# A norm's channel weight and rstd in one VectorE operation, and weight splits in four pieces, in a hybrid decoder block

## The chip, the core and the metric

The kernel runs on one core of a Trainium2 chip. The metric is device time in microseconds (us) of one execution. A core has five engines that run their own instruction queues and meet only at semaphores: TensorE (PE) multiplies matrices, VectorE (DVE), ScalarE (ACT) and GpSimd (POOL) work element by element, and SyncE (SP) issues transfers. Data lie in an on-chip memory of 128 partitions (SBUF) and in the accumulators of TensorE (PSUM).

## The reference

One decoder layer on 1024 tokens with 16 learned meta tokens in front (1040 rows of 1024 channels), in float32:

```python
h = jnp.concatenate([meta, x], axis=1)
mix = hybrid_mixer(rms_norm(h, g_pre_mix), w_in, ...)     # short convolution and stick-breaking attention
h = h + rms_norm(mix, g_post_mix)
ffn = conv_gated_mlp(rms_norm(h, g_pre_ffn), ...)
h = h + rms_norm(ffn, g_post_ffn)

def rms_norm(x, g):
    y = xf * lax.rsqrt(jnp.mean(xf * xf, axis=-1, keepdims=True) + RMS_EPS)
    return (y * g).astype(x.dtype)
```

The mixer multiplies the normalised rows by `w_in` (1024 x 8192), which yields the convolution's three inputs, q, k, v of 16 heads and two gates. Attention works on blocks of queries: with z the scaled scores, a weight is sigmoid(z) times the running product, from the query backwards, of 1 - sigmoid(z). The two branches are projected, gated, summed and multiplied by `w_out`. The MLP follows. The change touches the first norm and all products with `w_in` and the two branch projections.

## The kernel before

**Precision by splitting.** TensorE takes a rounded float type (F32R). Each operand is split into a high part, rounded by ScalarE, and a low part, the difference: `split` (L63 to L65) issues a copy on ScalarE (L64) and a subtraction (L65) on VectorE or, where asked, on GpSimd. A product is then three matmuls: high x high, high x low, low x high (L124 to L126). L64 and L65 are lines of a helper, so that in the profile they are told apart by their tiles: `whi`, `wlo` for weights, `ah`, `al` for attention weights, `vv` for values, `xnT` for the normalised rows.

**Dense products.** `Dense` runs a list of 80 items (64 column blocks of `w_in`, 8 of each branch projection). An item has one weight block of 128 x 1024. `load` (L96) fetches it on SP's queue into `raw`, `prep` (L103) splits it into `whi` and `wlo`, with the subtraction on GpSimd, and `run` (L112) does 3 chunks of tokens with 8 x 3 matmuls each; at the start of item i, item i+1 is prepared and the load of i+2 issued. `raw`, `whi` and `wlo` have two buffers each.

**The start.** `x_block(b)` norms 128 rows (the ninth block has 16): ScalarE squares and sums (L456), `rstd_of` (L67 to L77) makes 1/sqrt by a ScalarE square root and five one-column VectorE operations, the rows are weighted (L458 to L462), and `to_features` (L174) transposes them on TensorE (L179) in two groups of four, each split by ScalarE and VectorE into `xnT`. In blocks 0 to 2 the weighting is one VectorE operation, x times rstd times channel weight (L459); in the later blocks GpSimd multiplies by the channel weight (L461) and VectorE by rstd (L462). `start_items` interleaves the blocks with the chunks of the first two items.

**Attention.** For every pair of heads (8 pairs), `stage1` makes scores (L326, L327), two sigmoids on ScalarE (L328, L329), a running product by a VectorE scan over up to 1040 columns (L336), a product on GpSimd (L339), and a causal mask on GpSimd (L340). `stage2` transposes the weights on TensorE (L373), splits them into `ah` (ScalarE) and `al` (VectorE), and multiplies them with `vv` (L363, L364). Steps of the two stages alternate, and between them steps of the dense items are run at a rate that ends them with the pair. The convolution branch has two VectorE operations of 1026 columns per block (`conv3`, L196 to L199).

Each engine's queue is set when the kernel is built, by a scheduler that may move independent instructions past one another, so the order of the queues is near that of the code but not the same. After attention come the projections (to about 1260 us), `w_out` and the second norm, the up-projection and the down-projection, which the diff doesn't touch.

Of the kernel before, what the change touches and what calls it, by code (L numbers as in the profile page):

```python
# [8 lines left out]
F32 = mybir.dt.float32  # L9
F32R = mybir.dt.float32r  # L10
AF = mybir.ActivationFunctionType
ALU = mybir.AluOpType
# [3 lines left out]
D = 1024  # L16
# [16 lines left out]
def block_kernel(ctx, tc, x, meta_tokens, g_pre_mix, w_in, channels, w_proj_conv,  # L33
                 w_proj_attn, w_out, g_post_mix, g_pre_ffn, w_up_gate, w_down,
                 g_post_ffn, out):
    nc = tc.nc

    def pool(name, bufs=1, side="left", space=None):
        kw = dict(name=name, bufs=bufs, reuse_waits="tile")
        if space is not None:  # L40
            kw["space"] = space
        else:
            kw["side"] = side
        return tc.tile_pool(**kw)
# [18 lines left out]
    def split(hi, lo, src, lo_engine=None):  # L63
        nc.scalar.copy(hi, src)  # L64
        (lo_engine or nc.vector).tensor_tensor(lo, src, hi.bitcast(F32), op=ALU.subtract)  # L65

    def rstd_of(small, ssq, n):  # L67
        v = small.tile([P, 1], F32, name="v", tag="v")
        s = small.tile([P, 1], F32, name="s", tag="s")
        t = small.tile([P, 1], F32, name="t", tag="t")  # L70
        v, s, t, ssq = v[:n], s[:n], t[:n], ssq[:n]
        nc.vector.tensor_scalar(v, ssq, 1.0 / D, EPS, op0=ALU.mult, op1=ALU.add)
        nc.scalar.activation(s, v, AF.Sqrt)
        nc.vector.reciprocal(s, s)
        nc.vector.scalar_tensor_tensor(t, s, v, s, op0=ALU.mult, op1=ALU.mult)
        nc.vector.tensor_scalar(t, t, -0.5, 1.5, op0=ALU.mult, op1=ALU.add)
        nc.vector.tensor_tensor(s, s, t, op=ALU.mult)  # L77
        return s

    class Dense:  # L80
# [22 lines left out]
        def prep(self, i):  # L103
            if i < len(self.items) and i not in self.hl:
                self.load(i)
                raw = self.raw.pop(i)
                hi = wpool.tile([P, D], F32R, name="whi", tag="whi")
                lo = wpool.tile([P, D], F32R, name="wlo", tag="wlo")
                split(hi, lo, raw, nc.gpsimd)
                self.hl[i] = (hi, lo)  # L110

        def run(self, i):  # L112
# [61 lines left out]
    def to_features(dst_hi, dst_lo, src, n, pp):  # L174
        for j in range(2):
            tp = pp.tile([P, 512], F32, name="tp", tag="tp")
            for k in range(4):
                kb = 4 * j + k
                nc.tensor.transpose(tp[:, k * P:k * P + n], src[:n, kb * P:(kb + 1) * P],  # L179
                                    ident[:n, :n])  # L180
            tv = tp.rearrange("p (k n) -> p k n", k=4)[:, :, :n]
            split(dst_hi[:, 4 * j:4 * j + 4], dst_lo[:, 4 * j:4 * j + 4], tv)
# [231 lines left out]
    def start_items(x_block):  # L414
        gens = [dense.run(0), dense.run(1)]

        def chunk(i, n):
            for _ in range(n):
                next(gens[i], None)

        for c in range(3):
            for b in range(3):
                x_block(3 * c + b)
                if c > 0 and b < 2:
                    chunk(b, 8)
        chunk(0, 9)
        chunk(1, 9)

    with ExitStack() as p0:
        small = p0.enter_context(pool("p0s", 2, "right"))  # L430
        gb = work.tile([P, NT], F32, name="gb", tag="wk", bufs=4)[:, :D]
        junk = work.tile([P, NT], F32, name="junk", tag="wk", bufs=4)[:, :D]
        warm = small.tile([P, 1], F32, name="warm", tag="v")
        nc.vector.memset(warm, 1.0)
        nc.scalar.activation(warm, warm, AF.Sqrt)

        xts = {}

        def x_load(b):
            n = P if b < 8 else 16  # L440
            xt = work.tile([P, NT], F32, name="xt", tag="be", bufs=6)[:, :D]
            if b == 0:
                nc.sync.dma_start(xt[:NMETA, :], meta_tokens)
                nc.sync.dma_start(xt[NMETA:, :], x[:P - NMETA, :])
            elif b < 9:
                nc.sync.dma_start(xt[:n, :], x[P * b - NMETA:P * b - NMETA + n, :])
            xts[b] = xt

        def x_block(b):
            if b + 3 < 9:  # L450
                x_load(b + 3)
            n = P if b < 8 else 16
            xt = xts[b]
            xn = work.tile([P, NT], F32, name="xn", tag="fl")[:, :D]
            ssq = small.tile([P, 1], F32, name="ssq", tag="ssq")
            nc.scalar.activation((xn if b < 2 else junk)[:n], xt[:n], AF.Square, accum_out=ssq[:n])  # L456
            r = rstd_of(small, ssq, n)
            if b < 3:  # L458
                nc.vector.scalar_tensor_tensor(xn[:n], xt[:n], r, gb[:n], op0=ALU.mult, op1=ALU.mult)  # L459
            else:  # L460
                nc.gpsimd.tensor_tensor(xn[:n], xt[:n], gb[:n], op=ALU.mult)  # L461
                nc.vector.tensor_scalar(xn[:n], xn[:n], r, None, op0=ALU.mult)  # L462
            to_features(xnT[:, 0, :, b * P:b * P + n], xnT[:, 1, :, b * P:b * P + n], xn, n, ps_tp)

        x_load(0)
        nc.sync.dma_start(gb, g_pre_mix.partition_broadcast(P))
        x_load(1)
        x_load(2)
        dense.load(0)
        dense.load(1)  # L470
        nc.sync.dma_start(par, channels[:, :40])
        start_items(x_block)


# [553 lines left out]
    for k, _ in enumerate(products(0, *HALF[1], bank_of(ps_o, "po"), evac_u(*HALF[1]))):  # L1028
        if k % 2:
            next(prep, None)  # L1030
# [40 lines left out]
    for i in range(1, len(pairs)):  # L1071
        p, gate = divmod(i, 2)
        if gate:
            conv_gelu(p)
            sets = [products(i, 1, 512, bank, evac_g(p))]
        else:
            sets = [products(i, j0, n, bank, evac_u(j0, n)) for j0, n in HALF]
        for _ in prep:
            pass
        prep = prep_pair(i + 1) if i < last_pair else prep_down_first()  # L1080
        for si, st in enumerate(sets):
            for k, _ in enumerate(st):
                if gate or (7 * si + k) % 2:
                    next(prep, None)
# [45 lines left out]
    for gi, fbs in enumerate(groups):  # L1130
# [14 lines left out]
        for tb in range(8):  # L1145
# [3 lines left out]
            for hf in range(2):  # L1149
                ps = bank()  # L1150
                c = slice(hf * 512, (hf + 1) * 512)
# [6 lines left out]
                a = accs[tb][:, c]  # L1158
# [4 lines left out]
                if last:  # L1163
                    sq = dw.tile([P, 512], F32, name="sq", tag="sq", bufs=2)
                    nc.scalar.activation(sq, a, AF.Square, accum_out=ssqs[tb][:, hf:hf + 1])
                    eng = nc.vector if (tb == 7 and hf) else nc.gpsimd
                    eng.tensor_tensor(a, a, g_post2[:, c], op=ALU.mult)
            next(prep, None)
            if last:
                a, hb, s0 = accs[tb], hbs[tb], ssqs[tb]  # L1170
                nc.vector.tensor_tensor(s0[:, 0:1], s0[:, 0:1], s0[:, 1:2], op=ALU.add)
                r = rstd_of(fsml, s0[:, 0:1], P)
                for hf in range(2):
                    c = slice(hf * 512, (hf + 1) * 512)
                    nc.vector.scalar_tensor_tensor(a[:, c], a[:, c], r, hb[:, c],
                                                   op0=ALU.mult, op1=ALU.add)
# [58 lines left out]
```

## Time and profile before

| | us |
|---|---|
| median of 3 executions (2069.74 to 2076.77) | 2070.41 |
| the profiled execution | 2079.27 |
| its span, first to last instruction | 2077.1 |
| GpSimd busy (44%) | 914.8 |
| VectorE busy (50%) | 1033.7 |

The profile is of one execution, somewhat longer than the median. A row of its timeline is: start in the span, duration, engine, line, operation, output<-inputs, shapes, count of merged instructions and, in brackets, how long the engine had been idle and what ended that. A group's row gives the busy time of its instructions, the mean of one, and the idle time of the engine before them. A row of the waits is: engine, line, what it waited for, total, times, longest. An instruction that is held up after it has begun counts as busy, so a long duration can be a wait.

### The profile page before, as it was taken

How to read it: one execution, taken by the hardware profiler on the slowest of the kernel's cores; microseconds unless marked ns; L12 is line 12 of the kernel's file. 1: busy time of each engine (PE TensorE's matmuls, PEld its weight loads, DVE VectorE, ACT ScalarE, POOL GpSimd, SP SyncE). 2: the span in 40 equal slices, each digit the busy share in tenths (PEclk: the TensorE clock that was granted, in tenths of full speed). 3: DMA queues.
4: the chain of work that ended last, by engine and by line, in shares of the span. 5: the costliest groups of instructions: out<-in, count | busy, mean ns of one | idle time of the engine just before them, and what ended most of it. 6: DMA issues, size and time to landing. Idle time of an engine off the chain costs nothing.

```text
span 2077.1 us, 30701 instructions
## 1 busy us (share of the span) xinstructions
PE 1988.1 (96%) x12228; PEld 1860.9 (90%) x12228; DVE 1033.7 (50%) x1545; ACT 851.9 (41%) x1771; POOL 914.8 (44%) x764
## 2 busy tenths in 40 slices
PE   5999999999999999999999989979999999999997
PEld 5999999999999999999999989978898899878886
DVE  6445555555555555554232114685444444445546
ACT  4445454545444454545441113354334434412122
POOL 4444444434444444444212551225655656555353
PEclk9999999999999999999999999989999999999999
DMA  3111101111111101111475674313222122253323
GB/s 134 41 51 42 61 31 51 42 41 52 42 51 41 61 32 51 41 48 55 138 231 171 184 189 129 102 54 102 74 90 82 62 102 70 74 182 102 101 81 132
DMA packets 56171, 177.56 MB, mean 85 GB/s; under 512 B 12872, under 2 KB 12872, under 8 KB 56028
## 3 DMA queue, kind: packets, MB, share of 16 engines
q1 hardware_dynamic: 52704, 165.09, 24.5%
q10 hardware_dynamic: 3324, 10.50, 1.6%
q8 instruction: 96, 1.57, 0.3%
q14 instruction: 47, 0.39, 0.1%
HBM read 131.36 MB, written 44.21 MB: 85 GB/s over the span
## 4 chain that ended last, share of the span: by engine, by line
PE 74%; DVE 11%; DMA 6%; ACT 4%; POOL 3%; issue 2%; ACTq 0%; DVEq 0%; POOLq 0%; SPq 0%
PE mm L124 13%; PE mm L125 12%; PE mm L126 12%; PE st L863 6%; PE st L865 5%; PE st L867 5%; PE st L1157 3%; PE st L1155 3%; PE st L1156 3%; PE tp L373 3%; DVE fl L336 3%; PE av L363 2%; PE av L364 2%; DMA xv<-in_x_dram 2%; POOL a_op L65 2%
## 5 line engine op out<-in xcount | busy, mean ns | idle before, releaser
L124 PE MATMUL mm<-xnT,whi 128*128 128x342 f32 (+2 forms) x1536 | 506.8, 330 | 3.6 <-ACT xnT L64 3.6
L125 PE MATMUL mm<-xnT,whi 128*128 128x342 f32 (+2 forms) x1536 | 494.7, 322 | 0.5 <-DVE xnT L65 0.5
L126 PE MATMUL mm<-xnT,wlo 128*128 128x342 f32 (+2 forms) x1536 | 493.0, 321 | 0.0
L339 POOL TENSOR_TENSOR be<-be,fl 114x127 f32<-114x127 f32 (+2 forms) x144 | 178.3, 1238 | 372.3 <-DVE fl L336 350.9
L124 PEld LDWEIGHTS mm<-xnT,whi 128*128 128x128 f32 x1536 | 290.5, 189 | 8.3 <-ACT xnT L64 4.0
L125 PEld LDWEIGHTS mm<-xnT,whi 128*128 128x128 f32 x1536 | 291.1, 190 | 2.1 <-DVE xnT L65 1.0
L126 PEld LDWEIGHTS mm<-xnT,wlo 128*128 128x128 f32 x1536 | 290.5, 189 | 0.0
L336 DVE TENSOR_TENSOR_SCAN fl<-fl,upper 114x128 f32<-114x128 f32 (+2 forms) x144 | 228.0, 1585 | 117.6 <-ACT fl L328 102.8
L65 POOL TENSOR_TENSOR wlo<-raw,whi 128x1024 fp32r<-128x1024 f32 x80 | 191.5, 2394 | 203.5 <-ACT whi L64 203.5
L65 POOL TENSOR_TENSOR a_op<-raw,a_op 128x512 fp32r<-128x512 f32 (+1 forms) x136 | 193.6, 1436 | 88.6 <-ACT a_op L64 86.4
L65 DVE TENSOR_TENSOR al<-tp,ah 128x342 fp32r<-128x342 f32 (+4 forms) x288 | 127.3, 450 | 147.0 <-ACT ah L64 145.7
L64 ACT CAST ah<-tp 128x342 fp32r<-128x342 f32 (+4 forms) x288 | 112.7, 397 | 193.4 <-PE tp L373 185.1
L863 PE MATMUL st<-opT,a_op 128*128 128x258 f32 (+2 forms) x528 | 171.3, 324 | 2.3 <-ACT snap L878 1.1
L865 PE MATMUL st<-opT,a_op 128*128 128x258 f32 (+2 forms) x528 | 169.5, 321 | 2.4 <-DVE opT L65 1.5
L867 PE MATMUL st<-opT,a_op 128*128 128x258 f32 (+2 forms) x528 | 169.3, 321 | 0.0
L328 ACT ACTIVATE fl<-z 114x348 f32<-114x348 f32 (+10 forms) x240 | 111.3, 464 | 127.6 <-PE z L327 123.3
L64 ACT CAST a_op<-raw 128x512 fp32r<-128x512 f32 (+1 forms) x136 | 85.1, 633 | 152.6 <-DVE raw L775 46.0
L373 PE MATMUL tp<-ident,be 114*128 114x114 f32 x720 | 119.5, 263 | 27.7 <-DVE al L65 25.0
L1162 DVE TENSOR_TENSOR acc<-acc,st 128x512 f32<-128x512 f32 x144 | 98.5, 687 | 91.1 <-PE st L1157 91.1
L865 PE MATMUL st<-opB,a_op 128*128 128x512 f32 (+2 forms) x396 | 127.8, 323 | 1.8 <-DVE opB L65 1.8
L863 PE MATMUL st<-opB,a_op 128*128 128x512 f32 (+2 forms) x396 | 127.9, 323 | 0.0
L867 PE MATMUL st<-opB,a_op 128*128 128x512 f32 (+2 forms) x396 | 127.4, 322 | 0.0
(171 smaller groups left out, 4327.6 us busy)
## 6 DMA issues: line engine op xcount, KB each, us to landing
raw<-in_w_in_dram SPq DMA_DIRECT2D x64, 512.0 KB, 3.4
raw<-in_w_up_gate_dram SPq DMA_DIRECT2D x44, 512.0 KB, 3.5
act_d<-owork SPq DMA_DIRECT2D x22, 512.0 KB, 4.2
araw<-act_d SPq DMA_DIRECT2D x22, 512.0 KB
raw<-in_w_down_dram SPq DMA_DIRECT2D x22, 512.0 KB, 3.2
y_d<-yy SPq DMA_DIRECT2D x8, 513.0 KB
ga_d<-gt SPq DMA_DIRECT2D x8, 513.0 KB
o_d<-ot SPq DMA_DIRECT2D x8, 513.0 KB
```

The source lines that it names most:

```text
L64: nc.scalar.copy(hi, src)
L65: (lo_engine or nc.vector).tensor_tensor(lo, src, hi.bitcast(F32), op=ALU.subtract)
L124: nc.tensor.matmul(ps, wh, xh, start=(kb == 0), stop=False)
L125: nc.tensor.matmul(ps, wh, xl, start=False, stop=False)
L126: nc.tensor.matmul(ps, wl, xh, start=False, stop=(kb == KB - 1))
L328: nc.scalar.activation(fl[:, c0:c0 + n], z, AF.Sigmoid, scale=-0.125)
L336: nc.vector.tensor_tensor_scan(fl[:, :nk][:, ::-1], fl[:, :nk][:, ::-1], upper[:, NT - nk:][:, ::-1], 1.0, op0=ALU.mult, op1=ALU.max)
L339: nc.gpsimd.tensor_tensor(be[:, 0:nk - 1], be[:, 0:nk - 1], fl[:, 1:nk], op=ALU.mult)
L373: nc.tensor.transpose(tp[:n, QB * j:QB * (j + 1)], blocks[j][0][:, kb * P:kb * P + n], ident[:QB, :QB])
L863: nc.tensor.matmul(ps, wt[:, 0, k], xh, start=start and kb == 0, stop=False, skip_group_check=True)
L865: nc.tensor.matmul(ps, wt[:, 0, k], xl, start=False, stop=False, skip_group_check=True)
L867: nc.tensor.matmul(ps, wt[:, 1, k], xh, start=False, stop=stop and kb == 3, skip_group_check=True)
```

## The change

The first norm's weighting is the one VectorE operation in all nine blocks; GpSimd's multiplication and VectorE's second one go. In `prep`, GpSimd's subtraction of 1024 columns becomes four of 256 columns; ScalarE's copy stays whole. Other uses of `split` stay as they are.

```diff
                 hi = wpool.tile([P, D], F32R, name="whi", tag="whi")
                 lo = wpool.tile([P, D], F32R, name="wlo", tag="wlo")
-                split(hi, lo, raw, nc.gpsimd)
+                nc.scalar.copy(hi, raw)
+                for a in range(0, D, 256):
+                    c = slice(a, a + 256)
+                    nc.gpsimd.tensor_tensor(lo[:, c], raw[:, c], hi[:, c].bitcast(F32),
+                                            op=ALU.subtract)
                 self.hl[i] = (hi, lo)
...
             r = rstd_of(small, ssq, n)
-            if b < 3:
-                nc.vector.scalar_tensor_tensor(xn[:n], xt[:n], r, gb[:n], op0=ALU.mult, op1=ALU.mult)
-            else:
-                nc.gpsimd.tensor_tensor(xn[:n], xt[:n], gb[:n], op=ALU.mult)
-                nc.vector.tensor_scalar(xn[:n], xn[:n], r, None, op0=ALU.mult)
+            nc.vector.scalar_tensor_tensor(xn[:n], xt[:n], r, gb[:n], op0=ALU.mult, op1=ALU.mult)
```

## The prediction

> **What bounds the kernel now.** I read the page's head, then TensorE's waits, then busy time by stretch, then the timeline of the places where TensorE waits.
>
> ```profile
> span 2077.1 us, 30701 instructions
> PE 1988.1 (96%) x12228; PEld 1860.9 (90%) x12228; DVE 1033.7 (50%) x1545; ACT 851.9 (41%) x1771; POOL 914.8 (44%) x764
> ```
>
> TensorE is busy 1988.1 of 2077.1 us. No matmul is removed, so the change can win only part of the other 89 us, and what a lower clock costs. The waits of TensorE (total, times, longest) say where that idle time is, and two stretches say how much of it lies at the start and in the attention stage:
>
> ```profile
> PE tp L373 <- DVE al L65: 25.0, 22, 2.0
> PE tp L179 <- DVE xn L459: 18.1, 3, 9.5
> PE mm L124 <- DVE gal L615: 5.2, 1, 5.2
> PE mm L126 <- POOL wlo L65: 2.7, 3, 1.2
> PE tp L373 <- DVE vv L65: 2.4, 6, 0.4
> ...
> 23.78:60.00 36.22, 30.27 (x171) 28.34 (x171) 24.93 (x56) 13.80 (x33) 11.92 (x5) 0.91 0.00 1
> 100.00:1020.00 920.00, 892.11 (x5818) 858.84 (x5818) 493.21 (x680) 454.45 (x1039) 393.82 (x420) 1.00 0.14 48
> ```
>
> The columns of the last two rows are the stretch, its length, then busy time of PE, PEld, DVE, ACT and POOL, then TensorE's granted clock. In the attention stage TensorE idles 920 - 892.1 = 27.9 us, and 25.0 + 2.4 = 27.4 of that are waits of the transposes of L373 for VectorE's low halves. VectorE is busy only 493 of 920 us there, so it isn't short of time; it is late at single places. Two of them, with the engine, line and duration of each instruction:
>
> ```profile
> 235.48 2.39 POOL L65 TENSOR_TENSOR wlo<-raw,whi 128x1024 fp32r<-128x1024 f32 x1
> 235.70 4.34 DVE L336 TENSOR_TENSOR_SCAN fl<-fl,upper 114x1040 f32<-114x1040 f32 x1 [1.61 <-ACT fl L328]
> 239.97 0.90 DVE L65 TENSOR_TENSOR al<-tp,ah 128x342 fp32r<-128x342 f32 x2
> 240.51 0.51 PE L373 MATMUL tp<-ident,be 114*128 114x114 f32 x3 [1.48 <-DVE al L65]
> ...
> 218.18 2.40 POOL L65 TENSOR_TENSOR wlo<-raw,whi 128x1024 fp32r<-128x1024 f32 x1
> 218.79 2.87 DVE L198 SCALAR_TENSOR_TENSOR yy<-cc,par,yy 128x1026 f32<-128x1026 f32 x1 [1.47 <-ACT yy L197]
> 221.58 0.50 DVE L65 TENSOR_TENSOR al<-tp,ah 128x342 fp32r<-128x342 f32 x1
> 222.14 0.30 PE L373 MATMUL tp<-ident,be 114*100 114x114 f32 x1 [1.25 <-DVE al L65]
> ...
> 114.48 0.51 PE L373 MATMUL tp<-ident,be 114*128 114x114 f32 x3 [1.96 <-DVE al L65]
> 921.08 0.30 PE L373 MATMUL tp<-ident,be 114*100 114x114 f32 x1 [1.25 <-DVE al L65]
> 939.53 0.51 PE L373 MATMUL tp<-ident,be 114*128 114x114 f32 x3 [1.56 <-DVE al L65]
> ```
>
> The weight split holds something that the VectorE scan needs: the scan seems to run 4.34 us, but 2.17 of them (235.70 to 237.87) lie under GpSimd's split, and it ends 2.17 us after that. The first convolution step of L198 is held in the same way until 220.58. The low half `al`, which TensorE waits for, stands behind them in VectorE's queue. This comes back in every head pair: 8 times in the first form (first and last row 114.48 and 939.53; the eight idle times add up to 12.5 us) and 7 times in the second (first and last 222.14 and 921.08, sum 8.5). The other seven `al` waits and the six `vv` waits, 4.0 + 2.4 us, lie about 35 us later in each pair.
>
> **At the start** the same thing happens between the splits, the weighting of L461 and the norm chain:
>
> ```profile
> 13.82 4.67 POOL L65 TENSOR_TENSOR wlo<-raw,whi 128x1024 fp32r<-128x1024 f32 x2 [8.38 <-ACT whi L64]
> 15.82 0.38 DVE L75 SCALAR_TENSOR_TENSOR t<-s,v 128x1 f32<-128x1 f32 x1
> 16.42 2.09 DVE L77 TENSOR_TENSOR s<-s,t 128x1 f32<-128x1 f32 x1
> 18.45 2.34 POOL L461 TENSOR_TENSOR xn<-xt,gb 128x1024 f32<-128x1024 f32 x1
> 18.54 3.33 DVE L459 SCALAR_TENSOR_TENSOR xn<-xt,s,gb 128x1024 f32<-128x1024 f32 x1
> ...
> 37.50 2.38 DVE L75 SCALAR_TENSOR_TENSOR t<-s,v 128x1 f32<-128x1 f32 x1
> 37.52 2.34 POOL L461 TENSOR_TENSOR xn<-xt,gb 128x1024 f32<-128x1024 f32 x1 [3.25 <-DVE s L74]
> 23.78 0.95 PE L124 MATMUL mm<-xnT,whi 128*128 128x356 f32 x2
> ```
>
> A VectorE operation on one column takes 2.09 or 2.38 us because a 1024-wide GpSimd operation runs beside it. The row at 15.82 shows more: that operation began under the first of the two splits, ended at 16.20, and the second split ran on to 18.49. So VectorE got through **between two GpSimd instructions**. A second case, in the other direction:
>
> ```profile
> 274.00 1.21 POOL L339 TENSOR_TENSOR be<-be,fl 114x583 f32<-114x583 f32 x1 [1.38 <-ACT be L329]
> 274.55 2.12 DVE L336 TENSOR_TENSOR_SCAN fl<-fl,upper 114x698 f32<-114x698 f32 x1
> 275.28 1.47 POOL L340 TENSOR_SCALAR_AFFINE_SELECT be<-be 114x114 f32<-114x114 f32 x1
> ```
>
> GpSimd's product ends at 275.21, its next instruction is recorded at 275.28 and then takes 1.47 us, to 276.75, just past the scan's end at 276.67: the waiting scan went first.
>
> The Trainium skill, "SBUF — State Buffer", section "Who interferes with whom", calls this an exclusive lock on a port pair that VectorE and GpSimd share, held for a whole instruction; the first to start keeps it. The trace agrees (2.09 us for one column).
>
> **The change part by part.** Costs come from these groups (busy us, mean ns) and one line's min/median/max:
>
> ```profile
> L65 POOL TENSOR_TENSOR wlo<-raw,whi 128x1024 fp32r<-128x1024 f32 x80 | 191.5, 2394 | 203.5 <-ACT whi L64 203.5
> L65 POOL TENSOR_TENSOR w_o<-raw,w_o 128x672 fp32r<-128x672 f32 x1 | 1.5, 1522 | 0.0
> L65 POOL TENSOR_TENSOR w_o<-raw,w_o 128x336 fp32r<-128x336 f32 x1 | 0.9, 856 | 0.0
> L459 DVE SCALAR_TENSOR_TENSOR xn<-xt,s,gb x3: 1276/1284/3327, 8.1 to 18.5; 128x1024 f32<-128x1024 f32 x3
> 36.65 0.74 DVE L462 TENSOR_SCALAR xn<-xn,s 128x1024 f32<-128x1024 f32 x1
> L65 DVE TENSOR_TENSOR al<-tp,ah 128x342 fp32r<-128x342 f32 x191 | 96.3, 511 | 104.9 <-ACT ah L64 103.7
> ```
>
> *One piece of a split.* From 336 to 672 columns the time grows by 666 ns, 1.98 ns a column with 190 ns fixed, so 256 columns are estimated at 0.70 us. The bounds are a quarter of 2394 ns (0.60) and the 336-column row (0.86). Four pieces: 2.8 us instead of 2.4 (2.4 to 3.4).
>
> [...]
>
> *80 splits in pieces.* GpSimd gains 80 x 0.4 = 32 us of work; it is busy 394 of 920 us in the attention stage, so this is covered, and if it weren't, TensorE would wait for `wlo`, which it doesn't between 60 and 1020 us. Queued behind the pieces on GpSimd are the memset of `ql` and the product `be` (L339), and on SP's queue the next weight load, which waits for the last piece; these move back by up to 0.4 us plus the scan that goes ahead (2.2). TensorE has no wait for `be` in the list, so that cover stands.
>
> *Attention.* First form: the scan is ready at 235.70 and waits for a piece to end near 236.2 instead of 237.87, so `al` comes 1.7 us earlier against a wait of 1.48. Second form: L198 is ready at 218.79, the first piece ends near 218.9, so 1.7 us earlier against 1.25. The rest of the pieces then run under `al`, whose 191 instructions average 511 ns and are never held. So nearly all of 12.5 + 8.5 = 21.0 us can go. In the third place the scans and products follow so closely that a late piece pushes the next product and scan back by about as much (0.2 us won, 0.4 lost); I count nothing. What is late next is unknown; **I take 18**, with 0 to 27 as ends.
>
> *Start.* In block 2, L77 waits at most a piece (1.4 us won) and the combined operation of L459 finds no L461 beside it (3.33 to at most 1.28 + 0.7, 1.35 won or more): about 3 us earlier. From block 3 on, VectorE pays 1.28 instead of 0.74, 6 x 0.54 = 3.2 us more work, but GpSimd's six operations (2.4 us each) and the waits under them go, so that VectorE no longer waits 2.38 us at 37.50. TensorE's idle time from 23.78 to 60 is 36.22 - 30.27 = 5.95 us, and its clock there is 0.91, a loss of 3.3 us, part of which is the first warm-up that stays. I take 3 + 4.7 + 1.3 = **9**, between 3 (only block 2) and 12 (all of it). It can't be much more, since VectorE would then be near full: 24.9 us of work less some 3 of waits inside it, plus what the combined operation adds beyond the stretched L462 (about 1), is 23 in 27 us.
>
> *Projections.* The same splits run there, with TensorE waiting 2.7 us for `wlo` and 5.2 for a chain of transfers in which a split and a weight reload stand. The first piece comes 1.7 us earlier, the reload 0.4 later each time: 2.7 won to 16 x 0.4 = 6.4 lost. I take 0.
>
> **Sum:** 18 + 9 + 0 = 27. The profiled execution took 2079.27 us (its span plus about 2 around it), so it would be 2052; that execution is 8.9 above the median of 2070.41. Against the median: 2070.41 - 27 = **2043.4**.
>
> **Rivals.** (1) *Half of it comes back.* With the pieces, every scan beside a split meets up to four short holds, and VectorE's delay moves to scans that run free now. Half of the attention gain goes: 9 + 9, 2052. For it: the third place above. Against it: most `al` never meet the lock. (2) *Only the start gains.* The order of the queues at build time shifts and the scans fall on splits in new places: 2061. Nothing in the trace speaks for it beyond the closeness of the instructions. (3) *Slower: no hand-over between pieces.* If GpSimd's pieces follow so fast that VectorE can't get in, each hold lasts 2.8 us instead of 2.4: 28 waits x 0.4 = 11 more, projections 6 more, start 6 gained instead of 9: 2070.4 + 11 = 2081. It decides if the pause between pieces is shorter than what let VectorE in at 16.2 and 275.2; those two rows speak against it. (4) *The change doesn't do what it says*: L461 is gone, but the chain of small operations and the transposes bind the start: 3 instead of 9, 2049.
>
> **How the numbers follow.** Forecast (2032 to 2048) 0.60; rival 4 0.12; rival 1 0.14; rival 2 0.09; rival 3 0.05. The range goes from the attention gain at 27 with the start at 10 (2033) to just beyond rival 2 (2062). A measurement of this kernel can tell about 0.5% (10 us) from no change: above 2060 it counts as the same, above 2081 as slower. Faster 0.86, same 0.11, slower 0.03.
>
> **What would show it.** In the changed profile: `wlo` pieces near 0.70 us; the 1040-wide scans near 2.2 to 2.9 us and none at 4.3; L198 below 2.0; TensorE's `al` waits from 25.0 to under 8; no L461; the first projection matmul near 20.6 us instead of 23.8, and L77 and L75 never over 0.9. I'd be wrong if pieces run back to back under a scan that waits for all four, if new `al` waits of an equal sum stand elsewhere, or if TensorE waits for `wlo` or `be`.

## The result, and the profile after

| | before | after |
|---|---|---|
| median of 4 executions, us | 2073.59 (2069.74 to 2078.95) | 2044.13 (2042.38 to 2045.85) |
| span of the profiled execution | 2077.1 | 2044.2 |

The ratio is 0.9856, with a 95% interval of 0.9827 to 0.9885: 29.5 us less by the medians, 32.9 by the two profiled spans. The profiled execution of the kernel before (2079.27 us) was longer than any of the four in the table. The forecast was 2043.4.

The head of the page after, and its first groups that answer to the splits and the scans:

```profile
span 2044.2 us, 30953 instructions
PE 1982.2 (97%) x12228; PEld 1857.7 (91%) x12228; DVE 1006.6 (49%) x1545; ACT 851.5 (42%) x1771; POOL 997.5 (49%) x998
...
L112 POOL TENSOR_TENSOR wlo<-raw,whi 128x256 fp32r<-128x256 f32 x320 | 270.0, 876 | 208.0 <-ACT whi L109 207.9
L340 DVE TENSOR_TENSOR_SCAN fl<-fl,upper 114x128 f32<-114x128 f32 (+2 forms) x144 | 215.6, 1499 | 117.0 <-ACT fl L332 103.0
```

GpSimd is busy 82.7 us longer and VectorE 27.1 us less: some of the waiting moved from one to the other, since a held instruction counts as busy. The line numbers of this kernel are four higher from `prep` to the first norm: L340 is the scan that was L336, L377 the transpose that was L373, L202 the convolution step that was L198; L462 is the norm's one VectorE operation. TensorE's waits after:

```profile
PE tp L183 <- DVE xn L462: 15.2, 3, 9.4
...
PE mm L128 <- DVE gal L615: 7.0, 1, 7.0
PE tp L377 <- DVE al L65: 5.8, 8, 2.0
...
PE tp L377 <- DVE vv L65: 0.2, 1, 0.2
```

The waits for `al` and `vv` fell from 27.4 to 6.0 us. The two places that the prediction showed, in the same pair of heads:

```profile
223.86 4.85 POOL L112 TENSOR_TENSOR wlo<-raw,whi 128x256 fp32r<-128x256 f32 x4
224.07 2.71 DVE L340 TENSOR_TENSOR_SCAN fl<-fl,upper 114x1040 f32<-114x1040 f32 x1 [1.61 <-ACT fl L332]
226.71 0.90 DVE L65 TENSOR_TENSOR al<-tp,ah 128x342 fp32r<-128x342 f32 x2
227.25 0.51 PE L377 MATMUL tp<-ident,be 114*128 114x114 f32 x3
...
208.09 4.87 POOL L112 TENSOR_TENSOR wlo<-raw,whi 128x256 fp32r<-128x256 f32 x4
208.71 1.29 DVE L202 SCALAR_TENSOR_TENSOR yy<-cc,par,yy 128x1026 f32<-128x1026 f32 x1 [1.47 <-ACT yy L201]
```

The scan takes 2.71 us where it took 4.34, the convolution step 1.29 where it took 2.87, and the transpose at 227.25 has no idle time before it. Now GpSimd is the one that is held: its four pieces last 4.85 us together, because the scan stands between them.

Where the time went, by marks in the two profiles: first scores matmul at 76.5 and 66.1 us, first product with `yT` at 1062.3 and 1027.8, first up-projection product at 1363.2 and 1326.8, end of the span at 2077.1 and 2044.2. So the start won 10.4 us, the attention stage 24.1, the projections and second norm 1.9, and the rest, which the change doesn't touch, is 3.5 longer. Start and attention in busy time by stretch, before and then after:

```profile
0.00:76.50 76.50, 52.41 (x300) 49.36 (x301) 43.56 (x92) 32.61 (x68) 28.36 (x21) 0.96 0.29 105
76.50:1062.30 985.80, 956.70 (x6230) 922.77 (x6229) 516.07 (x717) 486.94 (x1109) 416.73 (x442) 1.00 0.17 56
```

```profile
0.00:66.10 66.10, 49.40 (x300) 46.58 (x301) 37.82 (x92) 32.66 (x68) 16.88 (x27) 1.00 0.34 121
66.10:1027.80 961.70, 953.54 (x6231) 923.39 (x6230) 493.24 (x717) 486.98 (x1109) 504.72 (x625) 1.00 0.17 57
```

In the attention stage TensorE's idle time falls from 29.1 to 8.2 us, and its busy time by another 3.2 us for one recorded instruction more.

### The profile page after: what moved, and what is told of

Same layout as the page of the kernel before. It is cut to its first block, busy times and chain, and to the rows that moved or that the text cites. A ratio compares the mean times of both kernels' runs of the same rounds, so it can differ in the third digit from the quotient of the medians.

```text
span 2044.2 us, 30953 instructions
## 1 busy us (share of the span) xinstructions
PE 1982.2 (97%) x12228; PEld 1857.7 (91%) x12228; DVE 1006.6 (49%) x1545; ACT 851.5 (42%) x1771; POOL 997.5 (49%) x998
## 4 chain that ended last, share of the span: by engine, by line
PE 79%; DVE 8%; DMA 6%; ACT 3%; POOL 2%; issue 2%; ACTq 0%; DVEq 0%; SPq 0%; POOLq 0%
PE mm L128 13%; PE mm L129 13%; PE mm L130 13%; PE st L863 6%; PE st L867 6%; PE st L865 6%; PE tp L377 3%; PE st L1155 3%; PE st L1157 3%; PE st L1156 3%; PE av L367 2%; PE av L368 2%; DMA xv<-in_x_dram 2%; PE z L331 2%; PE z L330 2%
## 5 line engine op out<-in xcount | busy, mean ns | idle before, releaser
L112 POOL TENSOR_TENSOR wlo<-raw,whi 128x256 fp32r<-128x256 f32 x320 | 270.0, 876 | 208.0 <-ACT whi L109 207.9
L343 POOL TENSOR_TENSOR be<-be,fl 114x127 f32<-114x127 f32 (+2 forms) x144 | 181.0, 1257 | 284.0 <-DVE fl L340 268.0
L340 DVE TENSOR_TENSOR_SCAN fl<-fl,upper 114x128 f32<-114x128 f32 (+2 forms) x144 | 215.6, 1499 | 117.0 <-ACT fl L332 103.0
L377 PE MATMUL tp<-ident,be 114*128 114x114 f32 x720 | 119.0, 263 | 6.8 <-DVE al L65 5.8
```

The source lines that it names most:

```text
L112: nc.gpsimd.tensor_tensor(lo[:, c], raw[:, c], hi[:, c].bitcast(F32), op=ALU.subtract)
L340: nc.vector.tensor_tensor_scan(fl[:, :nk][:, ::-1], fl[:, :nk][:, ::-1], upper[:, NT - nk:][:, ::-1], 1.0, op0=ALU.mult, op1=ALU.max)
L343: nc.gpsimd.tensor_tensor(be[:, 0:nk - 1], be[:, 0:nk - 1], fl[:, 1:nk], op=ALU.mult)
L377: nc.tensor.transpose(tp[:n, QB * j:QB * (j + 1)], blocks[j][0][:, kb * P:kb * P + n], ident[:QB, :QB])
```

## The experiments

The theory: a VectorE operation with two inputs in SBUF is held until the GpSimd instruction that runs beside it ends, and gets in before the next one; TensorE waits where such an operation stands in front of the low halves. (Two inputs are not the whole condition: L462 of the kernel before has one such tensor, takes 746 ns in the median, and took 2994 beside L461.) Each experiment changes the kernel after unless it says otherwise. All stage lengths are from the profiles; "attention" runs from the first scores to the first product with `yT`.

| kernel | a piece, ns (median) | first scores | attention | `al` + `vv` waits, us | median, us | ratio to before (95%) |
|---|---|---|---|---|---|---|
| before | 2396 | 76.5 | 985.8 | 27.4 | 2073.6 | |
| norm only | 2396 | 66.7 | 986.0 | 27.5 | 2067.8 | 0.9961 (0.9946 to 0.9977) |
| pieces only | 739 | 72.7 | 963.2 | 5.8 | 2054.4 | 0.9900 (0.9884 to 0.9917) |
| after (both) | 739 | 66.1 | 961.7 | 6.0 | 2044.1 | 0.9856 (0.9827 to 0.9885) |
| two pieces | 1292 | 65.8 | 976.2 | 16.6 | 2060.5 | 0.9934 (0.9920 to 0.9949) |
| eight pieces | 463 | 65.2 | 956.8 | 2.4 | 2036.7 | 0.9820 (0.9801 to 0.9838) |
| sixteen pieces | 325 | 65.1 | 958.6 | 3.2 | 2042.8 | 0.9874 (0.9852 to 0.9897) |
| every fourth column | 1177 | 68.6 | 971.6 | 10.7 | 2061.8 | 0.9965 (0.9950 to 0.9980) |
| whole first, then pieces | 2.4 us + 4 pieces | 66.9 | 990.8 | 27.9 | 2066.5 | 0.9990 (0.9978 to 1.0001) |
| fills first, then pieces | 739 | 65.3 | 958.1 | 2.8 | 2034.0 | 0.9828 (0.9804 to 0.9852) |
| low part on VectorE | 1226 | 66.3 | 961.8 | 4.2 | 2034.5 | 0.9827 (0.9809 to 0.9845) |
| eight, then VectorE | 463 and 1226 | 64.1 | 956.8 | 2.4 | 2030.1 | 0.9810 (0.9784 to 0.9836) |
| before, norm in pieces | 2396 | 71.5 | 987.4 | 27.5 | 2068.7 (one execution) | |

(The waits are those between 100 and 1010 us, at the transposes and, where there are any, at the products behind them. In the medians, the kernel before was 2068 to 2074 us in the several comparisons; ratios are to its own runs beside each.)

### The two halves of the change alone

Norm only has the split whole again:

```diff
-                nc.scalar.copy(hi, raw)
-                for a in range(0, D, 256):
...
+                split(hi, lo, raw, nc.gpsimd)
```

Pieces only has the weighting of the kernel before:

```diff
-            nc.vector.scalar_tensor_tensor(xn[:n], xt[:n], r, gb[:n], op0=ALU.mult, op1=ALU.mult)
+            if b < 3:
+                nc.vector.scalar_tensor_tensor(xn[:n], xt[:n], r, gb[:n], op0=ALU.mult, op1=ALU.mult)
+            else:
+                nc.gpsimd.tensor_tensor(xn[:n], xt[:n], gb[:n], op=ALU.mult)
+                nc.vector.tensor_scalar(xn[:n], xn[:n], r, None, op0=ALU.mult)
```

> Splits whole again, norm in one VectorE operation. Theory (VectorE is held for the length of the GpSimd instruction beside it, and gets in only between two of them): the two parts act in different stages, so this one wins only at the start. TensorE's al waits in the attention stage stay near 25 us; the first scores come near 68 us (before 76.5, after 66.1), since in block 2 the one-column operation L77 is still held 2 us by a whole split; total 7 to 9 us less than before. Rival (the start's gain comes from the pieces): first scores near 74 us, total within 3 us of before.

> Splits in four pieces, norm as before (GpSimd multiplies in blocks 3 to 8). Theory: al waits near 6 us as in the changed kernel, attention stage (first scores to first matmul on yT) near 962 us instead of 986; first scores near 74 us, as only block 2 gains; total 23 to 27 us less than before. Rival (the queues' new order made the gain): al waits and stage time somewhere else, since the order at the start differs from the changed kernel's.

The norm alone leaves the attention stage as it was (986.0 us, the `al` waits 25.0) and brings the first scores to 66.7; the pieces alone bring the attention stage to 963.2 and the first scores to 72.7. By stages of the profiles both are what the theory said, and the rivals fall: the pieces do the same for the attention stage in a kernel whose start is ordered otherwise. Both totals fell short of what was expected: by the medians the norm alone took 5.3 us less, not 7 to 9, and the pieces alone 18.7, not 23 to 27. At the start the two don't add: 9.8 and 3.8 us alone, 10.4 together. The norm alone still has L77 held by a whole split, in VectorE's timeline:

```profile
15.80 2.21 DVE L77 TENSOR_TENSOR s<-s,t 128x1 f32<-128x1 f32 x1
18.05 1.28 DVE L458 SCALAR_TENSOR_TENSOR xn<-xt,s,gb 128x1024 f32<-128x1024 f32 x1
```

But the combined operation behind it is free, and so are the blocks after it.

### Two, eight and sixteen pieces

For two pieces (eight have 128 columns, sixteen 64):

```diff
-                for a in range(0, D, 256):
-                    c = slice(a, a + 256)
+                for a in range(0, D, 512):
+                    c = slice(a, a + 512)
```

> As the changed kernel, but two pieces of 512 columns. Theory: a hold lasts at most 1.25 us instead of 0.74; at the two places of each pair VectorE is released 1.1 us earlier than before, against waits of 1.48 and 1.25, so some 0.1 to 0.4 us are left of each: al waits 7 to 12 us, total 2 to 6 us above the changed kernel. If the number of openings counted and not the length of a hold, half of the attention gain would be lost: al waits near 16, total 10 us above it.

> As the changed kernel, but eight pieces of 128 columns, about 0.45 us each, 3.6 us of GpSimd a split. Theory: holds are shorter still, but little is left to win: al waits 3 to 6 us, total within 3 us of the changed kernel. Rival (each piece is a new hold for VectorE, and GpSimd's extra 64 us come back as late products): al waits above 8 us and the total 5 us or more above the changed kernel.

> As the changed kernel, but sixteen pieces of 64 columns, about 0.32 us each by the line through 0.45 (128) and 0.73 (256), 5.1 us of GpSimd a split. Theory: nothing is left to win in the attention stage (2.4 us of al waits with eight pieces), so the stage stays within 2 us of 957; GpSimd's 80 x 1.4 us more shows only where it is near its bound, in the projections: total 0 to 6 us above eight pieces (2036.7).

With two pieces less is won than the arithmetic of one release gave: 16.6 us of waits remain and the total is 16 above four pieces, not 2 to 6. In each pair 0.4 to 0.6 us is left at each of the two places, now partly at the product L368, and the third place grew a little. The rows of TensorE's waits between 100 and 1010 us:

```profile
PE tp L377 <- DVE al L65: 9.3, 16, 1.9
PE av L368 <- DVE al L65: 4.0, 7, 0.6
PE tp L377 <- DVE vv L65: 3.3, 6, 0.6
```

Eight pieces were expected to end within 3 us of four; they took 7 less by the medians, with intervals of the ratios that just overlap, and 4.9 us less in the attention stage. The same view for eight pieces has one row:

```profile
PE tp L377 <- DVE al L65: 2.4, 3, 1.3
```

With sixteen, nothing more is won in the attention stage (958.6 against 956.8), and the total is 6 us above eight by the medians and some 11 by the two ratios; by the profiles the projections take 4.0 us more (300.9 against 296.9). Three waits are left in the attention stage with eight pieces and with sixteen. The first pair's wait at the transpose falls on, to 1.96, 1.28 and 0.92 us with four, eight and sixteen pieces. But another wait, 16 to 18 us behind it, which the kernel before doesn't have, grows: 0.27, 0.86 and 2.05 us. There a product `be` (L343) stands behind a whole split of 3.30, 3.88 or 5.08 us in GpSimd's queue, ScalarE's next sigmoid waits for GpSimd's write to `be` behind that product, the scan waits for the sigmoid, and `al` and the transpose follow. With sixteen pieces:

```profile
113.24 5.08 POOL L112 TENSOR_TENSOR wlo<-raw,whi 128x64 fp32r<-128x64 f32 x16 [4.89 <-ACT whi L109]
118.27 0.42 POOL L343 TENSOR_TENSOR be<-be,fl 114x127 f32<-114x127 f32 x1
118.72 0.47 ACT L332 ACTIVATE fl<-z 114x356 f32<-114x356 f32 x1 [4.38 <-POOL be L349]
119.22 1.15 DVE L340 TENSOR_TENSOR_SCAN fl<-fl,upper 114x356 f32<-114x356 f32 x1 [4.39 <-ACT fl L332]
120.83 0.51 PE L377 MATMUL tp<-ident,be 114*128 114x114 f32 x3 [2.05 <-DVE al L65]
```

So the waits fall with the length of one hold, 2396, 1292, 739, 463 ns, until hardly any are left, while GpSimd's own time for a split grows from 2.4 to 3.7 us (8 x 463 ns) and 5.2 (16 x 325 ns) and in the end delays its own products.

### Is it the hold, or something else that pieces bring?

Two kernels add GpSimd work to each of the 64 splits of `w_in` ahead of the four pieces, of about equal length, and differ in whether it reads. Whole first:

```diff
                 nc.scalar.copy(hi, raw)
+                if i < 64:
+                    nc.gpsimd.tensor_tensor(lo, raw, hi.bitcast(F32), op=ALU.subtract)
```

Fills first:

```diff
                 nc.scalar.copy(hi, raw)
+                if i < 64:
+                    for _ in range(2):
+                        nc.gpsimd.memset(lo.bitcast(F32), 0.0)
```

> As the changed kernel, but for the 64 blocks of w_in GpSimd computes the low part in one whole subtraction first and then a second time in the four pieces: the same values, nothing else depends on them, 2.4 us more of GpSimd each. Theory: the whole instruction holds VectorE as it did before, so al waits are back at 22 us or more and the attention stage near 985 us, although the four openings are still there behind it. Rival (order, or the openings alone): al waits near 6 and the stage near 962 us.

> As the changed kernel, but for the 64 blocks of w_in GpSimd first fills the low part with zeros twice (about 0.95 us each) and then computes it in four pieces; the fills only write. Theory, by the memset of ql that runs beside a scan in the profile of before: a fill holds nothing, so al waits stay near 6 us and the stage near 962 us, with 64 x 1.9 us more on GpSimd. Rival (GpSimd being late is what costs): al waits above 12 us.

With the whole subtraction first, the attention stage is 990.8 us and the waits are back; with the fills it is 958.1. The same place of the same pair, GpSimd and VectorE, first with the whole subtraction, then with the fills:

```profile
213.39 2.40 POOL L111 TENSOR_TENSOR wlo<-raw,whi 128x1024 fp32r<-128x1024 f32 x1
214.00 2.88 DVE L204 SCALAR_TENSOR_TENSOR yy<-cc,par,yy 128x1026 f32<-128x1026 f32 x1 [1.47 <-ACT yy L203]
```

```profile
206.56 1.97 POOL L112 MEMSET wlo<- 128x1024 f32 x2
207.19 1.29 DVE L205 SCALAR_TENSOR_TENSOR yy<-cc,par,yy 128x1026 f32<-128x1026 f32 x1 [1.47 <-ACT yy L204]
```

In both the VectorE operation begins about 0.6 us into GpSimd's work, and nothing that it reads or writes has to do with that work. Beside 2.40 us that read it takes 2.88, beside 1.97 that only write it takes 1.29; over the eight pairs of heads these are 2.49 to 2.88 and 1.29 each time. So it is the hold, it comes with an instruction that also reads, and neither 1.9 us more of GpSimd's time nor four openings by themselves decide. VectorE and GpSimd thus meet not only at semaphores, as the opening says of all engines. The Trainium skill, "SBUF — State Buffer", section "Who interferes with whom", says that a VectorE instruction with two SBUF inputs contends with a GpSimd instruction that reads SBUF and not with one that only writes it; these two rows agree. The fills themselves aren't stretched either, while a piece in the same kernel lasted up to 2766 ns:

```profile
L112 POOL MEMSET wlo<- x128: 945/955/965, 2.4 to 1002.0; 128x1024 f32 x128
```

The third kernel of this kind spreads each piece over all columns, so that no matmul can start on part of the low half:

```diff
-                for a in range(0, D, 256):
...
+                lv, rv, hv = [t.rearrange("p (n f) -> p n f", f=4) for t in (lo, raw, hi.bitcast(F32))]
+                for a in range(4):
+                    nc.gpsimd.tensor_tensor(lv[:, :, a], rv[:, :, a], hv[:, :, a], op=ALU.subtract)
```

> As the changed kernel, but piece a takes the columns a, a+4, a+8 and so on, so that every piece touches all eight blocks of the weights and no matmul can use the low part before the last piece ends. Theory (a hold ends with each GpSimd instruction): if a strided piece takes as long as the plain one (0.74 us), al waits stay near 6 us and the total within 3 us of the changed kernel. Rival (the gain is that the low part's first quarter is ready earlier): TensorE's waits for wlo or for al come back, total 10 us or more above the changed kernel.

A piece with a stride took 1177 ns, so the condition of the first line was not met, and the total of 2061.8 decides nothing by itself. Its 10.7 us of waits lie between those of 739 and 1292 ns. TensorE's waits for `wlo` in this kernel, of which 1.6 us are at the start, 6.9 in the projections and none in the attention stage:

```profile
PE mm L130 <- POOL wlo L112: 8.5, 5, 3.0
```

That an earlier first quarter plays no part in the attention stage rests on this and on the wait for `wlo` that is missing there in every kernel.

### What gained at the start

The kernel before, with GpSimd's multiplication in four pieces:

```diff
-                nc.gpsimd.tensor_tensor(xn[:n], xt[:n], gb[:n], op=ALU.mult)
+                for a in range(0, D, 256):
+                    nc.gpsimd.tensor_tensor(xn[:n, a:a + 256], xt[:n, a:a + 256], gb[:n, a:a + 256],
+                                            op=ALU.mult)
```

> The kernel before (splits whole), but GpSimd's multiplication by the channel weight in blocks 3 to 8 is four pieces of 256 columns; VectorE's multiplication by rstd stays. It asks whether the start gained by shorter holds or because a GpSimd step of 2.4 us left the chain of each block. Theory (both): holds in the norm chain fall below 0.8 us, but each block still waits for 2.8 us of GpSimd; first scores between 70 and 74 us (before 76.5, norm alone 66.7). Rival (holds alone): near 67 us. Rival (the chain alone): 76 us or later.

The first scores come at 71.5. By one profiled execution of each kernel, shorter holds are then worth 5.0 us of the norm's 9.8, and the rest comes with the one VectorE operation; here GpSimd's step is still in the chain, and VectorE waits for it:

```profile
30.27 1.21 DVE L464 TENSOR_SCALAR xn<-xn,s 128x1024 f32<-128x1024 f32 x1 [1.46 <-POOL xn L462]
```

The one total, 2068.7 us beside 2068.5 for the kernel before, doesn't show these 5 us.

### Two versions with shorter medians

The low part on VectorE, in place of the copy and the loop:

```diff
-                nc.scalar.copy(hi, raw)
-                for a in range(0, D, 256):
...
+                split(hi, lo, raw, nc.vector)
```

Eight pieces, then VectorE:

```diff
-                for a in range(0, D, 256):
...
+                eng, w = (nc.gpsimd, 128) if i < 64 else (nc.vector, D)
+                for a in range(0, D, w):
+                    c = slice(a, a + w)
+                    eng.tensor_tensor(lo[:, c], raw[:, c], hi[:, c].bitcast(F32), op=ALU.subtract)
```

> As the changed kernel, but the low part of the weights is one subtraction of 1024 columns on VectorE, none on GpSimd. Theory: no weight split holds VectorE any more, but each is 1.28 us of VectorE's own, in its queue before the attention's low halves: at the places where GpSimd's whole split cost 1.25 to 1.5 us of waiting, some 0 to 1 us each come back, and VectorE has 80 x 1.28 = 102 us more work in all. Al waits 8 to 16 us, total 5 to 15 us above the changed kernel. If VectorE's queue has room everywhere, al waits under 5 and the total below the changed kernel's.

> One VectorE operation in the norm; low parts in eight GpSimd pieces for the 64 blocks of w_in, and whole on VectorE for the 16 projection blocks, where GpSimd and transfers bound the work (from the first product with yT to the first with op: 297 us with eight pieces, 291 with VectorE). Theory: the two gains add, since they lie in different stages: 65 + 957 + 291 + 715 = 2028 span, about 2030 us, 5 to 8 below eight pieces. Rival (the stages after it give it back): 2035 or more.

The main forecast for VectorE was wrong and its last sentence right. One subtraction on VectorE takes about half as long as GpSimd's (1226 against 2396 ns), and no split on GpSimd is left that could hold VectorE; at the first place it runs while VectorE would wait for ScalarE anyway:

```profile
221.84 1.82 DVE L65 TENSOR_TENSOR wlo<-raw,whi 128x1024 fp32r<-128x1024 f32 x1 [0.42 <-ACT whi L64]
223.59 2.39 DVE L336 TENSOR_TENSOR_SCAN fl<-fl,upper 114x1040 f32<-114x1040 f32 x1
```

The attention stage is as long as with four pieces (961.8), and the projections to the first up-projection product take 291.1 us instead of 299.0, without the 7.0 us wait for `gal`. The combination took 2030.1 us, the lowest median of all. Its profile, of the shortest of its four executions, gives 64.1 + 956.8 + 287.7 + 714.7 by stages. The intervals of both ratios overlap that of the kernel after, the combination's only a little. How much the projections gave is less sure than the attention stage: three kernels that have the same code there (before, norm only, norm in pieces) took 300.9, 298.2 and 292.4 us for it.

## Why the prediction was right

**What bounds.** Right. TensorE's idle time fell with no matmul changed, and the chain from split to scan to `al` to transpose held in each experiment.

**A piece.** Estimated 0.70 us, measured 0.74, so that a split costs GpSimd 0.56 us more, not 0.4. GpSimd has that time: 1.9 us of fills more for each split cost the attention stage nothing. But the products that the prediction called covered are not so without limit, as sixteen pieces showed.

**Attention, 18 us taken, 24.1 measured.** The mechanism was right and the size was off. The ceiling of the two forms, 21.0, was nearly reached: of 15 waits only the first pair's 1.96 us remained, and three of 0.2 to 0.3 us are new, at a place some 14 to 16 us behind the first form. The third place, counted at nothing, won 3.2 of its 6.4 us: three of the seven pairs have no wait there any more, the others keep 0.5 to 1.0. And 3.2 us came from TensorE's busy time, which the sum left out. Of matmuls that follow each other freely, each starts 0.16 us after one that is recorded with 0.32, so that half of it lies under the next:

```profile
238.55 0.32 PE L125 MATMUL mm<-xnT,whi 128*128 128x342 f32 x1
238.71 0.32 PE L126 MATMUL mm<-xnT,wlo 128*128 128x342 f32 x1
```

The next one in the prediction's rows, the transpose at 240.51, starts only after the last of these has ended. There are 28 such waits before and 9 after; 19 x 0.16 is an estimated 3.0 us.

**Rival 1 exists, in one place.** In the first pair, where two convolution steps and a scan follow each other, each meets a piece, and TensorE's wait stays as long as it was (1.96 us before and after):

```profile
96.78 5.82 POOL L112 TENSOR_TENSOR wlo<-raw,whi 128x256 fp32r<-128x256 f32 x4
97.78 1.52 DVE L202 SCALAR_TENSOR_TENSOR yy<-cc,par,yy 128x1026 f32<-128x1026 f32 x1 [1.47 <-ACT yy L201]
99.22 2.85 DVE L340 TENSOR_TENSOR_SCAN fl<-fl,upper 114x1040 f32<-114x1040 f32 x1
102.00 1.68 DVE L203 SCALAR_TENSOR_TENSOR yy<-cc,par,yy 128x1026 f32<-128x1026 f32 x1
104.16 0.51 PE L377 MATMUL tp<-ident,be 114*128 114x114 f32 x3 [1.96 <-DVE al L65]
```

**Start, 9 taken, 10.4 measured.** Right, by the steps named: L75 and L77 in block 2 take 0.81 and 0.47 us instead of 0.38 and 2.09, L459's successor 1.72 instead of 3.33, the first projection matmul comes at 20.89 (20.6 was named), TensorE's clock to the first scores is 1.00 instead of 0.96. Of the 10.4 us, 7.4 are idle time of TensorE and 3.0 its busy time; the clock's term had been taken at 1.3. That VectorE's dearer operation would be covered held: TensorE's waits from 24 to 60 us, 5.9 us before, are 1.4 in all.

**Projections, 0 taken, 1.9 measured**, inside the scatter given above. The waits for `wlo` (2.7) went, and the wait behind the chain of transfers grew from 5.2 to 7.0.

**Rivals 2, 3 and 4** fell. VectorE gets in between pieces in each profile that has them (rival 3), the norm alone wins 9.8 us at the start and not 3 (rival 4), and the stage's gain is nearly the same with another order at the start (rival 2; 22.6 and 24.1 us).

**The total.** That 2044.13 came within 1 us of the forecast 2043.4 is in part luck. The three stages won 36.4 us by the profiles where 27 were taken, the untouched stages gave 3.5 back, and both the profiled execution of before and its median in this comparison (2073.59) lie above the 2070.41 from which the forecast was counted.

**What stays open:** the 3.5 us by which the untouched stages after the first up-projection product are longer. They take 713.9 us before and 714.0 to 720.4 in the other twelve profiles, so that the profiled execution of before was the shortest of the lot there; no run was made to tell scatter from a cause. Open, too, is how much of the start's 10.4 us is the change: the stage lengths of before come from one long execution. For the attention stage two kernels with the same code there confirm them (986.0 and 987.4 us); for the start none does, and the norm alone saved 5.3 us in the total where its start is 9.8 us shorter.

## What to carry to other kernels

A long duration of a VectorE instruction can be a GpSimd instruction beside it: compare one shape's shortest and longest duration before calling VectorE slow. GpSimd, off the critical path, cost here by the length of its single instructions far more than by its load. So cut such an engine's work into pieces about as short as the slack of the operation that they meet, or let it write only, or move the work to an engine with room at that place. Check the waits pair by pair afterwards: a chain of held operations meets each piece anew, and with many pieces the engine's own later work comes late.

## What the runs showed of the hardware that was not expected

GpSimd's subtraction on 128 partitions took 325, 463, 739, 1292 and 2396 ns for 64, 128, 256, 512 and 1024 columns (medians of 160 to 1280 instructions, of 80 for the last): about 187 ns and 2.16 ns a column, a straight line over the whole range. Taking every fourth column made the same 256 columns cost 1177 ns instead of 739:

```profile
L112 POOL TENSOR_TENSOR wlo<-raw,whi x320: 1147/1177/3242, 13.5 to 1223.4; 128x256 fp32r<-128x256 f32 x160
```

And with eight pieces in a split, GpSimd instructions of under half a microsecond back to back, VectorE still got in between them: the longest piece in that kernel lasted 2522 ns, 2.06 us more than the usual 463, about the length of a long scan.
